# Gate and up of 20 row pairs as block products of seven, two pairs direct, and the down projection in one group of 22 over rows kept in DRAM

## The chip, the cores and the metric

One core of a Trainium2 chip runs the kernel. The time is that of the device in microseconds (us), the median of several executions. PE is TensorE, DVE is VectorE, ACT is ScalarE, POOL is GpSimd; SP issues all DMAs of this kernel, in one queue.

## The reference, cut to what matters

All is float32, 1024 prompt rows and 8 sample rows (T = 1032 columns in the kernel, which keeps everything transposed, features on partitions).

```python
merged = sum(gates[:, :, n] * (br @ w_branch[n]) for n, br in enumerate((a_out, s_out, c_out)))
h = layer_norm(ALPHA * x + merged @ w_out, ln1_g, ln1_b)          # ALPHA = 2 ** 0.25
gt, up = jnp.split(h @ w_gate_up, 2, axis=-1)                      # 1024 x 2 * 2816
h = layer_norm(ALPHA * h + (jax.nn.silu(gt) * up) @ w_down, ln2_g, ln2_b)   # 2816 x 1024
```

Before these lines stand the combined input projection, a gated linear recurrence and two attentions.

## The kernel before

**Three matmuls per product.** Every operand is split into a high part in the matmul's format and a low rest: `split` (L69-73) is one cast on ACT and one subtraction on DVE. A product takes high x high, high x low, low x high (`mm3`, L100-109), each with a 128 x 128 stationary tile. A list-scheduling planner orders each engine's instructions at build time by the order of the code and by when buffers come free; on the chip each queue then runs in that order.

**Weights.** `half_raw` (L80) loads 512 columns (256 KB) into one of 6 buffers; `half_pair` gives 5 high and 4 low buffers for its split. `weights` does this for a whole row tile.

**The projection** (`project`, to 677 us) already multiplies in blocks of seven. Two row tiles of weights (a pair) and the inputs are cut in 2 x 2 blocks; seven products of sums of blocks stand for eight (`fast_quarter`, `fast_step`, L222-279). Each product runs over two quarters of 258 columns, 4 k tiles and 3 matmuls; the weights' sums and splits are made three steps ahead.

**Branches and out projection.** Each of the three branches loads its input rows from DRAM (`load_branch`, L116) in three column chunks of 384, 384 and 264, multiplies by its weights and adds into `M`. The last one leaves `merged` split in the slots of pool `slots0`. `out_proj` (L993) runs chunk by chunk over 8 output tiles with w_out held in `slots1`, adds ALPHA x, and starts the chunk's `layer_norm`, whose steps are issued between later products (`norm_step`). Its `emit` writes h split into `slots0`, and POOL leaves ALPHA h in `accs`.

**The feed-forward part** (`ffn`, L1030). For each of 22 pairs `gate_up` makes gate and up, 8 k tiles each, per chunk, and the gated row tile, split, stays in `slots1`. As 22 do not fit, there are three groups of 8, 7 and 7 pairs (`FPARTS`). After each of the first two, w_down's columns of that group are loaded once and the partial products of all chunks are added to `accs` (tiles `d`). The last group's w_down is held in `slots0` (tiles `dl`) and run chunk by chunk, with the second norm's steps in between; the last chunk has its own `last_layer_norm` (L932), and the second chunk's norm has a late step that follows it (L987-989).

Of the kernel before, what the change touches and what calls it, by code (L numbers as in the profile page):

```python
# [18 lines left out]
P = 128  # L19
# [5 lines left out]
CH = ((0, 384), (384, 384), (768, 264))  # L25
# [28 lines left out]
class Builder:  # L54
# [61 lines left out]
    def load_branch(self, br, c):  # L116
# [3 lines left out]
        for k in range(KT):  # L120
            hi, lo = (self.slot(e, c, f"b{br}{e}{k}_{c}", br == "s") for e in "HL")
            self.nc.sync.dma_start(lo.bitcast(F32), self.scr[br][:, k, t0:t0 + n])
            self.split(hi, lo, lo.bitcast(F32))
            act[k][c] = (hi, lo)


    def setup(self):
# [10 lines left out]
        nc.vector.memset(self.shift.bitcast(F32), -2.0 / 256)  # L138
# [83 lines left out]
    def fast_quarter(self, st, i):  # L222

        nc, ((a11, a12), (a21, a22)), u = self.nc, st["raw"], st["u"]
        if i in (1, 2, 4, 5):
            src = self.w1.tile([P, D // 2], F32, tag="sum", name=f"us{u}_{i}", bufs=3)
# [357 lines left out]
    def product(self, step, br, m, c, wb, gate):  # L584
# [11 lines left out]
        if step == 2:  # L596
            hi, lo = (self.slot(e, c, f"m{e}{m}_{c}", 0) for e in "HL")
# [288 lines left out]
    def col_mean(self, s, n, name):  # L886

        nc = self.nc
        hi = self.ph.tile([P, 384], F32R, tag="lh", name=f"{name}h", bufs=1)[:, :n]
        lo = self.ph.tile([P, 384], F32R, tag="ll", name=f"{name}l", bufs=1)[:, :n]  # L890
# [6 lines left out]
    def layer_norm(self, c, r, s1, gcol, emit, name, late=False):  # L897
# [6 lines left out]
        s2 = ph.tile([P, 384], F32, tag="s2", name=f"{name}s2{c}", bufs=1)[:, :n]  # L904
        for m in range(KT):
            nc.vector.tensor_sub(r[m], r[m], mu)
            sq = s2 if m == 0 else ph.tile([P, 384], F32, tag="sq", name=f"{name}sq{c}_{m}", bufs=2)[:, :n]
# [5 lines left out]
        rs = ph.tile([P, 384], F32, tag="rs", name=f"{name}rs{c}", bufs=1)[:, :n]  # L913
# [18 lines left out]
    def last_layer_norm(self, n, r, product, gcol, emit):  # L932
# [4 lines left out]
        tile_ = lambda tag, name, bufs, dt=F32: ph.tile([P, 384], dt, tag=tag, name=name, bufs=bufs)[:, :n]  # L937
# [16 lines left out]
        for m in range(KT):  # L954
# [6 lines left out]
            nc.vector.scalar_tensor_tensor(r[m], ps, 0.5, r[m], op0=ALU.mult, op1=ALU.add)  # L961
# [4 lines left out]
            elif m == LATE - 1:  # L966
# [4 lines left out]
                for k in range(LATE):  # L971
                    nc.vector.scalar_tensor_tensor(r[k], c0, 0.5, r[k], op0=ALU.mult, op1=ALU.add)
# [20 lines left out]
    def out_proj(self, merged):  # L993
        nc, io, ph = self.nc, self.io, self.ph
        self.accs = [self.acc.tile([P, T], F32, tag="acc", name=f"acc{m}", bufs=8) for m in range(KT)]
        h = [[None] * 3 for _ in range(KT)]
        self.norm = None
        w = [None] * KT
        for c, (t0, n) in enumerate(CH):
            s1 = ph.tile([P, 384], F32, tag="s1", name=f"o1s{c}", bufs=1)[:, :n]  # L1000
            rs = []
            for m in range(KT):
                if c == 0:
                    w[m] = self.resident(io["wout"][m], KT, f"wo{m}", 1)
# [3 lines left out]
                xr = ph.tile([P, 384], F32, tag="xres", name=f"xres{m}_{c}", bufs=3)[:, :n]  # L1008
# [10 lines left out]
            def emit(m, v, c=c):  # L1019
                bias = self.vec[:, V_B1 + m:V_B1 + m + 1]  # L1020
                hi, lo = (self.slot(e, c, f"h{e}{m}_{c}", 0) for e in "HL")
                nc.scalar.activation(hi, v, AF.Identity, bias=bias)
                nc.vector.scalar_tensor_tensor(lo, v, bias, hi.bitcast(F32), op0=ALU.add, op1=ALU.subtract)  # L1023
# [4 lines left out]
        return h  # L1028

    def ffn(self, h):  # L1030
        nc, io, ph = self.nc, self.io, self.ph

        def gate_up(f, c, wg, wu, j):
            t0, n = CH[c]
            pg = self.mm_tile(wg, h, c, f"fg{f}_{c}", tag=("s", "t")[c % 2])
            self.norm_step()
            t = ph.tile([P, 384], F32, tag="gt", name=f"ft{f}_{c}", bufs=3)[:, :n]
            nc.scalar.activation(t, pg, AF.Tanh, scale=0.5)  # L1038
            nc.vector.scalar_tensor_tensor(t, t, 1.0, pg, op0=ALU.add, op1=ALU.mult)  # L1039
            pu = self.mm_tile(wu, h, c, f"fu{f}_{c}")  # L1040
            nc.vector.tensor_mul(t, t, pu)  # L1041
            hi, lo = (self.slot(e, c, f"g{e}{f}_{c}", 1) for e in "HL")
# [235 lines left out]
```

## Time and profile before

| | us |
|---|---|
| median of 3 runs | 2026.82 |
| lowest, highest | 2025.91, 2030.33 |
| span of the profiled execution | 2027.6 |

How the time divides, by the first starts of the tiles named:

| stage | from, us |
|---|---|
| projection | 6.1 |
| attentions with branches a and c | 681.4 |
| branch s | 1077.2 |
| out projection | 1167.6 |
| gate and up of 8 pairs | 1259.8 |
| down of the first group | 1445.1 |
| down of the last group | 1928.6 |
| end | 2027.6 |

The page gives busy time by engine and groups of instructions; the views used below are the windows (busy time of each engine in a stretch), the timeline (instructions in order of time) and the tiles. A row of the timeline has the start, the length, the engine, the line, the operation, what it writes and reads, the shape, and in brackets how long the engine sat idle before it and what released it.

### The profile page before, as it was taken

The numbers are of one execution on the slowest core, as the hardware profiler recorded it, in microseconds if no ns is written. First come the engines' busy times: TensorE is split into PE (matmuls) and PEld (weight loads), VectorE is DVE, ScalarE is ACT, GpSimd is POOL, SyncE is SP. The second block draws the span as 40 slices with busy tenths as digits, with TensorE's granted clock in tenths as the row PEclk, the third lists the DMA queues.
The fourth block names the chain that finished last, engine by engine and source line by source line (L and its number), as shares of the span: only waits on it lengthen the run. The fifth ranks groups of instructions, "written<-read, shape, count | busy, mean of one in ns | idle before, by whom it ended". The sixth has DMA issues, their size and how long they took to land.

```text
span 2027.6 us, 35380 instructions
## 1 busy us (share of the span) xinstructions
PE 1963.3 (97%) x13732; PEld 1930.0 (95%) x13732; DVE 1204.2 (59%) x2565; ACT 879.1 (43%) x1922; POOL 125.3 (6%) x164
## 2 busy tenths in 40 slices
PE   6899999999999999999999999999999999999997
PEld 5899999999999898988999999999999999999996
DVE  8597888777676555389886568533322332223357
ACT  5456565555656455388774244422201221122324
POOL 3000010100000000012110003100000000000001
PEclk8999999999999999999999999999999999999999
DMA  4365455462333676567525241111211111111102
GB/s 173 129 227 181 153 186 170 144 228 82 118 131 114 234 240 215 158 170 204 155 72 174 85 145 30 43 42 43 58 47 43 42 57 41 57 45 43 56 28 84
DMA packets 140439, 235.41 MB, mean 116 GB/s; under 512 B 17280, under 2 KB 69584, under 8 KB 140240
## 3 DMA queue, kind: packets, MB, share of 16 engines
q1 hardware_dynamic: 140272, 233.17, 36.2%
q8 instruction: 107, 1.75, 0.4%
q14 instruction: 60, 0.49, 0.1%
HBM read 179.95 MB, written 55.23 MB: 116 GB/s over the span
## 4 chain that ended last, share of the span: by engine, by line
PE 86%; DVE 6%; DMA 3%; ACT 3%; issue 1%; SPq 0%; ACTq 0%; DVEq 0%; POOL 0%; POOLq 0%
PE ub L245 5%; PE ub L244 5%; PE ub L246 5%; PE fg L105 4%; PE fg L106 4%; PE fg L107 4%; PE fu L107 4%; PE fu L105 4%; PE fu L106 4%; PE d L105 3%; PE d L107 3%; PE d L106 3%; PE ud L246 2%; PE ud L245 2%; PE ud L244 2%; PE brs L105 1%
## 5 line engine op out<-in xcount | busy, mean ns | idle before, releaser
L105 PE MATMUL fg<-hH,wfg_h 128*128 128x384 f32 (+1 forms) x528 | 168.3, 319 | 3.0 <-DVE acc L1012 1.7
L106 PE MATMUL fg<-hL,wfg_h 128*128 128x384 f32 (+1 forms) x528 | 167.7, 318 | 0.4 <-DVE hL L1023 0.4
L107 PE MATMUL fu<-hH,wfu_l 128*128 128x384 f32 (+1 forms) x528 | 167.7, 318 | 0.0
L106 PE MATMUL fu<-hL,wfu_h 128*128 128x384 f32 (+1 forms) x528 | 167.6, 317 | 0.0
L105 PE MATMUL fu<-hH,wfu_h 128*128 128x384 f32 (+1 forms) x528 | 167.5, 318 | 0.0
L107 PE MATMUL fg<-hH,wfg_l 128*128 128x384 f32 (+1 forms) x528 | 167.5, 317 | 0.0
L1041 DVE TENSOR_TENSOR ft<-ft,fu 128x384 f32<-128x384 f32 (+1 forms) x66 | 33.8, 513 | 139.1 <-PE fu L107 139.1
L105 PE MATMUL d<-gH,wd_h 128*128 128x384 f32 (+1 forms) x360 | 114.4, 318 | 0.0
L106 PE MATMUL d<-gL,wd_h 128*128 128x384 f32 (+1 forms) x360 | 114.2, 317 | 0.0
L107 PE MATMUL d<-gH,wd_l 128*128 128x384 f32 (+1 forms) x360 | 114.2, 317 | 0.0
L1039 DVE SCALAR_TENSOR_TENSOR ft<-ft,fg 128x384 f32<-128x384 f32 (+1 forms) x66 | 33.8, 513 | 135.2 <-ACT ft L1038 132.9
L71 ACT CAST gH<-ft 128x384 fp32r<-128x384 f32 (+1 forms) x66 | 31.7, 481 | 175.0 <-DVE ft L1041 175.0
L105 PEld LDWEIGHTS fg<-hH,wfg_h 128*128 128x128 f32 x528 | 99.1, 188 | 3.9 <-DVE acc L1012 2.0
L106 PEld LDWEIGHTS fg<-hL,wfg_h 128*128 128x128 f32 x528 | 99.2, 188 | 1.0 <-DVE hL L1023 0.9
L107 PEld LDWEIGHTS fg<-hH,wfg_l 128*128 128x128 f32 x528 | 99.3, 188 | 0.0
L107 PEld LDWEIGHTS fu<-hH,wfu_l 128*128 128x128 f32 x528 | 99.2, 188 | 0.0
L105 PEld LDWEIGHTS fu<-hH,wfu_h 128*128 128x128 f32 x528 | 99.2, 188 | 0.0
L106 PEld LDWEIGHTS fu<-hL,wfu_h 128*128 128x128 f32 x528 | 99.2, 188 | 0.0
L1061 DVE SCALAR_TENSOR_TENSOR acc<-d,acc 128x384 f32<-128x384 f32 (+1 forms) x48 | 24.8, 516 | 108.4 <-PE d L107 108.4
L1038 ACT ACTIVATE ft<-fg 128x384 f32<-128x384 f32 (+1 forms) x66 | 30.1, 456 | 134.8 <-PE fg L107 134.8
L244 PE MATMUL ub<-th,u_0h 128*128 128x258 f32 x240 | 69.4, 289 | 7.5 <-ACT th L71 6.1
L244 PE MATMUL ud<-th,u_1h 128*128 128x258 f32 x240 | 70.2, 293 | 6.3 <-ACT u_1h L71 5.2
(957 smaller groups left out, 6872.4 us busy)
## 6 DMA issues: line engine op xcount, KB each, us to landing
ur<-win SPq DMA_DIRECT2D x120, 256.0 KB, 3.6
dck<-cmk SPq DMA_DIRECT2D x32, 256.0 KB, 3.6
dcv<-cmvT SPq DMA_DIRECT2D x32, 256.0 KB, 4.5
st<-scr_q SPq DMA_DIRECT2D x32, 256.0 KB, 5.2
scr_g<-za SPq DMA_DIRECT2D x12, 516.0 KB, 5.8
scr_g<-zb SPq DMA_DIRECT2D x12, 516.0 KB, 3.7
x<-xQ SPq DMA_DIRECT2D x8, 516.0 KB
scr_a<-ge SPq DMA_DIRECT2D x8, 516.0 KB
```

The lines of the kernel that those rows point to most:

```text
L71: ins = self.nc.scalar.copy(hi, src).ins
L105: nc.tensor.matmul(ps, sh, mh, start=i == 0, stop=False)
L106: nc.tensor.matmul(ps, sh, ml, start=False, stop=False)
L107: self.last_mm = nc.tensor.matmul(ps, sl, mh, start=False, stop=closes and i == last).ins
L244: mm(sh[:, w], xh, start=opens and k == 0, stop=False)
L245: mm(sh[:, w], xl, start=False, stop=False)
L246: self.last_mm = mm(sl[:, w], xh, start=False, stop=k == 3).ins
L1038: nc.scalar.activation(t, pg, AF.Tanh, scale=0.5)
L1039: nc.vector.scalar_tensor_tensor(t, t, 1.0, pg, op0=ALU.add, op1=ALU.mult)
L1041: nc.vector.tensor_mul(t, t, pu)
L1061: nc.vector.scalar_tensor_tensor(a, ps, 0.5, a, op0=ALU.mult, op1=ALU.add)
```

## The change

- The chunks become 388, 386 and 258 columns; the last is one quarter.
- h, merged and the inputs of branches a and c are kept in fixed tiles `HL` (774 columns and a tail of 258) instead of slots. The first norm's `emit` leaves h itself in `accs`, without POOL; ALPHA is multiplied where down adds.
- Pairs 0 and 1 are multiplied directly, in four quarters, right behind the out projection (`direct_units`). Beside them `h_sums` makes the sums of blocks of h and splits them.
- Pairs 2 to 21 are block products of seven (`units`, `unit_step`) with `fast_quarter`'s sums of weights.
- Gated rows are stored to a DRAM tensor `f`. `down` loads them again (`rows`), 22 for the first chunk and then 3 per product, splits them, and multiplies all 22 k tiles in one group per chunk and output tile; w_down is loaded and split again for every chunk (`streamed`).

```diff
-CH = ((0, 384), (384, 384), (768, 264))
+CH = ((0, 388), (388, 386), (774, 258))
 ...
-FPARTS = ((0, 8), (8, 7), (15, 7))
+DIRECT = (0, 1)
 ...
-LAST_CH = ((0, 0, 384), (1, 0, 384), (2, 0, 264))
 ...
+    def hl(self, k, t0, n):
+        cut = CH[2][0]
+        main, tail = self.HL[k]
+        return [a[:, t0 - cut:t0 - cut + n] for a in tail] if t0 >= cut else [a[:, t0:t0 + n] for a in main]
 ...
+            if br == "s":
+                hi, lo = (self.slot(e, c, f"b{br}{e}{k}_{c}", 0) for e in "HL")
+            else:
+                hi, lo = self.hl(k, t0, n)
 ...
-        nc.vector.memset(self.shift.bitcast(F32), -2.0 / 256)
+        nc.vector.memset(self.shift.bitcast(F32), -1.0 / 256)
 ...
-            hi, lo = (self.slot(e, c, f"m{e}{m}_{c}", 0) for e in "HL")
+            hi, lo = self.hl(m, t0, n)
 ...
-            nc.vector.scalar_tensor_tensor(r[m], ps, 0.5, r[m], op0=ALU.mult, op1=ALU.add)
+            nc.vector.scalar_tensor_tensor(r[m], r[m], ALPHA, ps, op0=ALU.mult, op1=ALU.add)
 ...
-                    nc.vector.scalar_tensor_tensor(r[k], c0, 0.5, r[k], op0=ALU.mult, op1=ALU.add)
+                    nc.vector.tensor_add(r[k], c0, r[k])
 ...
-            def emit(m, v, c=c):
-                bias = self.vec[:, V_B1 + m:V_B1 + m + 1]
-                hi, lo = (self.slot(e, c, f"h{e}{m}_{c}", 0) for e in "HL")
-                nc.scalar.activation(hi, v, AF.Identity, bias=bias)
-                nc.vector.scalar_tensor_tensor(lo, v, bias, hi.bitcast(F32), op0=ALU.add, op1=ALU.subtract)
-                nc.gpsimd.tensor_scalar(v, v, bias, ALPHA, op0=ALU.add, op1=ALU.mult)
-                h[m][c] = (hi, lo)
+            def emit(m, v, t0=t0, n=n):
+                hi, lo = self.hl(m, t0, n)
+                nc.scalar.activation(v, v, AF.Identity, bias=self.vec[:, V_B1 + m:V_B1 + m + 1])
+                self.split(hi, lo, v)
 
             self.norm_start(self.layer_norm(c, rs, s1, V_G1, emit, "n1"))
 ...
+    def direct_units(self):
+        nc, io = self.nc, self.io
+        def held(src, n, name):
+            out = []
+            for e in range(2):
+                raw = self.half_raw(src[:, e * 512:(e + 1) * 512], 512, f"{name}r{e}_")
+                hi, lo = (self.tp.tile([P, HT], F32R, tag="t", name=f"{name}{x}{e}_", bufs=32)[:, :512] for x in "hl")
+                self.split(hi, lo, raw)
+                out += [(hi[:, i:i + P], lo[:, i:i + P]) for i in range(0, 512, P)]
+            return out
+        def piece(f, q, wg, wu):
+            o = slice(q * QN, (q + 1) * QN)
+            act = [self.hl(k, q * QN, QN) for k in range(KT)]
+            pg, pu = (self.bank(tag, f"f{x}{f}_{q}")[:, :QN] for tag, x in ((("s", "t")[q % 2], "g"), ("mm", "u")))
+            self.mm3(pg, list(zip(wg, act)))
             self.norm_step()
+            t = self.w1.tile([P, QN], F32, tag="gt", name=f"ft{f}_{q}", bufs=2)
             nc.scalar.activation(t, pg, AF.Tanh, scale=0.5)
             nc.vector.scalar_tensor_tensor(t, t, 1.0, pg, op0=ALU.add, op1=ALU.mult)
+            self.mm3(pu, list(zip(wu, act)))
+            nc.vector.scalar_tensor_tensor(t, pu, 0.5, t, op0=ALU.mult, op1=ALU.mult)
+            nc.sync.dma_start(self.scr["f"][:, f, o], t)
+        w = {}
+        for f in DIRECT:
+            make = self.weights if f == 0 else held
+            w[f] = [make(io["wgu"][x + f], D, f"wf{x}_{f}") for x in (0, NF)]
+        self.ht = [[None] * 4 for _ in range(7)]
+        for n, m, q in ((0, 0, 0), (3, 4, 0), (5, 4, 2)):
+            self.ht[n] = [[self.hl(m + k, (q + p) * QN, QN) for p in range(2)] for k in range(4)]
+        for q in range(4):
+            for f in DIRECT:
+                piece(f, q, *w[f])
+            yield
+    def h_sums(self, i):
+        nc = self.nc
+        def pair(i, k, src, sign=1.0):
+            hi, lo = (self.tp.tile([P, HT], F32R, tag="t", name=f"h{i}_{k}{x}", bufs=32) for x in "hl")
+            self.ht[i][k] = [(hi[:, o:o + QN], lo[:, o:o + QN]) for o in (0, QN)]
+            (self.split if sign > 0 else partial(self.split_scaled, scale=sign))(hi, lo, src)
+        wide = lambda name, k: self.cb.tile([P, HT], F32, tag="w", name=f"{name}{k}", bufs=6)
+        x = lambda kh, th, k: self.accs[4 * kh + k][:, th * HT:(th + 1) * HT]
+        if i == 2:
+            self.t2 = [None] * 4
+        for k in range(4):
+            if i == 1:
+                t1 = wide("t1", k)
+                nc.vector.tensor_sub(t1, x(0, 0, k), x(0, 1, k))
+                pair(1, k, t1)
+            elif i == 2:
+                t3, t2 = wide("t3", k), wide("t2", k)
+                nc.vector.tensor_sub(t3, x(1, 1, k), x(0, 1, k))
+                nc.vector.tensor_add(t2, t3, x(0, 0, k))
+                pair(2, k, t2, -1.0)
+                pair(4, k, t3)
+                self.t2[k] = t2
+            else:
+                t4 = wide("t4", k)
+                nc.vector.tensor_sub(t4, self.t2[k], x(1, 0, k))
+                pair(6, k, t4)
+    def unit_step(self, st, i):
+        nc, f = self.nc, st["u"]
+        small = lambda tag, p: self.w2.tile([P, QN], F32, tag=tag, name=f"{tag}{f}_{p}", bufs=2)
+        for p in range(2):
+            if i == 0:
+                st["b", p] = self.bank("mm", f"fb{f}_{p}")[:, :QN]
+            elif i == 1:
+                st["d", p] = self.bank("t", f"fd{f}_{p}")[:, :QN]
+            elif i == 3:
+                st["c", p] = self.bank("s", f"fc{f}_{p}")[:, :QN]
+            b, c, d = st.get(("b", p)), st.get(("c", p)), st.get(("d", p))
+            ps = {0: b, 1: d, 2: b, 3: c, 4: b, 5: d, 6: b}[i]
+            opens = i in (0, 1, 3)
+            sh, sl = st["q", i]
+            mm = partial(nc.tensor.matmul, ps, skip_group_check=not opens)
+            for k in range(4):
+                w = slice(k * P, (k + 1) * P)
+                xh, xl = self.ht[i][k][p]
+                mm(sh[:, w], xh, start=opens and k == 0, stop=False)
+                mm(sh[:, w], xl, start=False, stop=False)
+                self.last_mm = mm(sl[:, w], xh, start=False, stop=k == 3).ins
+            if i == 3:
+                st["za", p], st["t", p] = (self.w2.tile([P, HT], F32, tag="z", name=f"{x}{f}_{p}", bufs=5) for x in ("za", "ft"))
+            za, t = st.get(("za", p)), st.get(("t", p))
+            lo_, hi_ = slice(0, QN), slice(QN, HT)
+            if i in (0, 1, 2):
+                st["s", i, p] = small(("p1s", "p5s", "u2s")[i], p)
+                if i == 1:
+                    nc.scalar.mul(st["s", i, p], ps, 0.5)
+                else:
+                    nc.scalar.copy(st["s", i, p], ps)
+            elif i == 3:
+                nc.vector.tensor_add(za[:, lo_], c, st["s", 0, p])
+            elif i == 4:
+                st["zb", p] = small("zb", p)
+                nc.vector.scalar_tensor_tensor(st["zb", p], b, -0.5, st["s", 1, p], op0=ALU.mult, op1=ALU.subtract)
+            elif i == 5:
+                nc.vector.tensor_add(za[:, hi_], d, st["s", 2, p])
+                nc.scalar.activation(t, za, AF.Tanh, scale=0.5)
+                nc.vector.scalar_tensor_tensor(t, t, 1.0, za, op0=ALU.add, op1=ALU.mult)
+                nc.vector.tensor_mul(t[:, hi_], t[:, hi_], st["zb", p])
+            else:
+                nc.vector.scalar_tensor_tensor(t[:, lo_], b, -0.5, t[:, lo_], op0=ALU.mult, op1=ALU.mult)
+                dst = self.scr["f"][:, f, :].rearrange("p (h q n) -> p h q n", h=2, q=2)[:, :, p, :]
+                nc.sync.dma_start(dst, t.rearrange("p (h n) -> p h n", h=2))
+    def units(self):
+        io, st = self.io, {}
+        def load(f):
+            st[f] = self.fast_load(f, io["wgu"][f], io["wgu"][NF + f])
+            st[f]["load"]((0, 0), (0, 1), (1, 0), (1, 1))
+        todo = [(f, i) for f in range(NF) if f not in DIRECT for i in range(7)]
+        ahead = 3
+        load(todo[0][0])
+        for f, i in todo[:ahead]:
+            self.fast_quarter(st[f], i)
+        yield
+        for n, (f, i) in enumerate(todo):
+            if i == 1 and f + 1 < NF:
+                load(f + 1)
+            if n + ahead < len(todo):
+                v, j = todo[n + ahead]
+                self.fast_quarter(st[v], j)
+            self.unit_step(st[f], i)
+            if i == 6:
+                del st[f]
+        yield
+    def streamed(self, m, act, ps, closes=True):
+        nc = self.nc
+        for k0 in range(0, NF, 4):
+            n = min(4, NF - k0)
+            w = self.weights(self.io["wdn"][m][:, k0 * P:(k0 + n) * P], n * P, f"wd{act[0][2]}_{m}_{k0}")
+            for j, (sh, sl) in enumerate(w):
+                k = k0 + j
+                mh, ml = act[k][:2]
+                nc.tensor.matmul(ps, sh, mh, start=k == 0, stop=False)
+                nc.tensor.matmul(ps, sh, ml, start=False, stop=False)
+                self.last_mm = nc.tensor.matmul(ps, sl, mh, start=False, stop=closes and k == NF - 1).ins
+    def rows(self, f, c):
+        t0, n = CH[c]
+        hi, lo = (self.gd.tile([P, CH[0][1]], F32R, tag="g", name=f"g{x}{f}_{c}", bufs=84)[:, :n] for x in "hl")
+        self.nc.sync.dma_start(lo.bitcast(F32), self.scr["f"][:, f, t0:t0 + n])
+        self.split(hi, lo, lo.bitcast(F32))
+        return hi, lo, c
+    def down(self):
+        nc, io, ph = self.nc, self.io, self.ph
+        self.norm = None
+        act = [[None] * NF for _ in CH]
+        pending = deque((f, c) for c in range(3) for f in range(NF))
+        def fetch(n):
+            for _ in range(n):
+                if pending:
+                    f, c = pending.popleft()
+                    act[c][f] = self.rows(f, c)
+        fetch(NF)
+        for c, (t0, n) in enumerate(CH):
             rs = [self.accs[m][:, t0:t0 + n] for m in range(KT)]
+            def product(m, last=True, c=c, n=n):
+                ps = self.bank(("mm", "s")[m % 2], f"dl{m}_{c}")[:, :n]
+                self.streamed(m, act[c], ps, last)
+                fetch(3)
                 return ps
 
             def emit(m, v, scale=1.0, t0=t0, n=n):
                 nc.scalar.activation(v, v, AF.Identity, bias=self.vec[:, V_B2 + m:V_B2 + m + 1], scale=scale)
                 nc.sync.dma_start(io["o_y"][:, m, t0:t0 + n], v)
 
+            if c == 2:
                 self.last_layer_norm(n, rs, product, V_G2, emit)
                 break
+            s1 = ph.tile([P, 388], F32, tag="s1", name=f"o2s{c}", bufs=1)[:, :n]
             for m, r in enumerate(rs):
                 ps = product(m)
                 if m in NORM_AT:
                     self.norm_step()
+                nc.vector.scalar_tensor_tensor(r, r, ALPHA, ps, op0=ALU.mult, op1=ALU.add)
                 if m == 1:
                     nc.vector.tensor_add(s1, rs[0], r)
                 elif m > 1:
                     nc.vector.tensor_add(s1, s1, r)
+            self.norm_start(self.layer_norm(c, rs, s1, V_G2, emit, "n2", c == 1))
 
 ...
+                  "q": [P, KT, 2, TP], "k": [P, 2, 2, TP], "v": [P, 8, 512], "f": [P, NF, T]}
 ...
+        self.sums = 2
 ...
+        with pool("acc") as self.acc:
+            with pool("slots0", "right") as slots0:
+                hy = ExitStack()
+                tails = [hy.enter_context(pool("hy")), slots0]
+                cut = CH[2][0]
+                self.HL = [([slots0.tile([P, cut], F32R, name=f"HL{k}{e}") for e in "hl"],
+                            [tails[k // 4].tile([P, T - cut], F32R, name=f"HT{k}{e}") for e in "hl"]) for k in range(KT)]
+                self.M = [self.acc.tile([P, T], F32, tag="acc", name=f"M{m}", bufs=8) for m in range(KT)]
 ...
                     self.load_branch("s", 0)
                     fill(4)
                     for _ in self.branch(2, "s"):
                         pass
+                with pool("ph5") as self.ph:
+                    self.out_proj(self.merged)
+                    late.close()
+                    self.tp = late.enter_context(pool("tp2", "right"))
+                    self.w1 = late.enter_context(pool("ea", "right"))
+                    direct = self.direct_units()
+                    next(direct)
+                with pool("cb") as self.cb:
+                    next(direct)
+                    self.h_sums(1)
+                    next(direct)
+                    self.h_sums(2)
+                    next(direct)
+                    units = self.units()
+                    next(units)
+                    self.h_sums(6)
+                hy.close()
+                with pool("w2") as self.w2:
+                    next(units)
+                late.close()
+            with pool("ph6") as self.ph, pool("gd", "right") as self.gd:
+                self.down()
```

More of the change, by code (lines that the diff above doesn't have):

```diff
@@ L1106, in build, with fill @@
             self.project()
+        self.sums = 2
         self.act, self.merged = {}, [[None] * 3 for _ in range(KT)]
[L1108 to L1124 removed]
+        with pool("acc") as self.acc:
[6 more added lines that the diff above has]
+                self.M = [self.acc.tile([P, T], F32, tag="acc", name=f"M{m}", bufs=8) for m in range(KT)]
+                with ExitStack() as gp:
+                    self.gp = gp.enter_context(pool("gp"))
+                    jobs = chain(self.branch(0, "a"), self.branch(1, "c"))
+                    def fill(n):
+                        for _ in range(n):
+                            next(jobs, None)
+                    with pool("ph1") as self.ph, pool("dp2") as self.dp:
+                        self.mem_attention(fill)
+                    with pool("ph2") as self.ph:
+                        self.windows(fill)
+                    late = ExitStack()
+                    self.slots = [late.enter_context(pool("slots1", "right"))]
                     self.load_branch("s", 0)
```

83 lines of the change are left out of this document (11 added, 72 removed).

## The prediction

> **What bounds the kernel now.** I read the page first (span, busy shares, the chain by engine), then the windows for the stages, the first and last starts of the tiles for where a stage ends, and the timeline for spacings. On the page, the span, the busy line and the chain by engine:
>
> ```profile
> span 2027.6 us, 35380 instructions
> ...
> PE 1963.3 (97%) x13732; PEld 1930.0 (95%) x13732; DVE 1204.2 (59%) x2565; ACT 879.1 (43%) x1922; POOL 125.3 (6%) x164
> ...
> PE 86%; DVE 6%; DMA 3%; ACT 3%; issue 1%; SPq 0%; ACTq 0%; DVEq 0%; POOL 0%; POOLq 0%
> ```
>
> PE is the bound in the mean. Whether it is in the stages that change, the windows tell (columns: PE, PEld, DVE, ACT, POOL busy, granted clock, DMA share, GB/s):
>
> ```profile
> 30.00:680.00 650.00, 632.42 (x5165) 627.42 (x5164) 495.97 (x1007) 360.46 (x680) 42.37 (x50) 0.99 0.45 152
> ...
> 1238.00:1300.00 62.00, 58.53 (x394) 56.65 (x393) 50.70 (x99) 30.40 (x59) 15.34 (x16) 1.00 0.10 30
> 1300.00:1445.00 145.00, 145.00 (x938) 145.00 (x937) 46.85 (x85) 34.16 (x66) 0.00 (x0) 1.00 0.16 47
> ...
> 1771.00:1928.00 157.00, 157.00 (x1007) 157.00 (x1006) 53.72 (x107) 39.70 (x85) 0.00 (x0) 1.00 0.17 49
> 1928.00:1990.00 62.00, 62.00 (x365) 62.00 (x364) 35.92 (x73) 16.03 (x35) 0.00 (x0) 1.00 0.14 47
> ```
>
> From 1300 to 1990 PE never rests, at full granted clock, while DMA is busy 14 to 17%. Fewer streamed columns there shorten the end one for one. The first row is the projection, which already multiplies in blocks of seven: there PE rests 17.6 of 650 us with DVE at 76%.
>
> **What a product costs.** A busy PE is not its rate, so I take starts of neighbours. In the timeline of PE, two half-products of a unit (258 columns) up to the next instruction, one out-projection product (384), and one down product (264):
>
> ```profile
> 300.96 0.28 PE L244 MATMUL ub<-th,u_2h 128*128 128x258 f32 x1
> ...
> 303.84 0.32 PE L105 MATMUL g<-xch,wgh 128*128 128x344 f32 x1
> ...
> 1201.00 0.35 PE L105 MATMUL op<-mH,wo0H 128*128 128x384 f32 x1
> ...
> 1205.18 0.34 PE L893 MATMUL n1mu0p<-n1mu0h,ones 128*128 128x384 f32 x1
> ...
> 2007.59 0.28 PE L105 MATMUL dl<-gH,wdl7H 128*128 128x264 f32 x1
> ...
> 2010.13 0.28 PE L959 MATMUL dl<-c0h,shift 128*128 128x264 f32 x1
> ```
>
> 24 matmuls in 2.88 us are 0.120 us each; 24 in 4.18 are 0.174; 21 in 2.54 are 0.121. The last gate-up group checks this; the starts of the two down tiles stand in their rows:
>
> ```profile
> L107 PE MATMUL d<-gH,wd_l x360: 282/334/337, 1445.5 to 1771.1; 128*128 128x384 f32 x120, 128*128 128x264 f32 x60
> ...
> L105 PE MATMUL dl<-gH,wdl0H x21: 281/334/346, 1928.6 to 1990.1; 128*128 128x384 f32 x14, 128*128 128x264 f32 x7
> ```
>
> Seven pairs take 1928.6 - 1771.1 - 0.1 = 157.4 us, 22.5 each; from spacings 48 x (0.174 + 0.174 + 0.121) = 22.5. They agree.
>
> **(a) Twenty pairs in blocks of seven.** A unit is 7 products x 2 column quarters x 4 k x 3 = 168 matmuls of 258 columns: 168 x 0.120 = 20.16 us. Gain 20 x (22.5 - 20.16) = **-46.8 us**.
>
> [...]
>
> **(b) Two direct pairs** go in quarters: 2 x 4 x 48 = 384 matmuls x 0.120 = 46.1 us for 45.0: **+1.1**.
>
> **(c) Widths 388, 386, 258** for 384, 384, 264. By the slope between 258 and 384 columns, (0.174 - 0.120) / 126, a set of three takes about 0.4705 us for 0.469. 528 sets in down, and some 768 before it (three branches and the out projection, 192 each): up to **+2**, at least 0.
>
> **(d) Do units keep 0.120?** DVE and ACT prices, from the last unit of the projection, which no side job disturbs, and the weights after it:
>
> ```profile
> 656.39 0.69 DVE L72 TENSOR_TENSOR u_3l<-ur,u_3h 128x512 fp32r<-128x512 f32 x1 [1.92 <-PE ub L246]
> ...
> 665.00 0.69 DVE L72 TENSOR_TENSOR u_6l<-ur,u_6h 128x512 fp32r<-128x512 f32 x1 [2.18 <-PE ub L246]
> 666.37 0.43 DVE L271 TENSOR_TENSOR za<-uc,p1s 128x258 f32<-128x258 f32 x1 [0.68 <-PE uc L246]
> ...
> 668.16 0.68 DVE L72 TENSOR_TENSOR wba_l<-wba0r__8961,wba_h 128x512 fp32r<-128x512 f32 x1
> ```
>
> Three steps in 8.61 us, 2.87 each, are 24 x 0.120: a unit alone runs at PE's pace. A new unit asks of DVE 4 sums and 7 splits at 0.69 and, for each of two quarters, five ops at 0.43 and one of 516 at about 0.69: 7.6 + 5.7 = 13.3 us of 20.16, 66%. Bounds 0 and the projection's idle share (2.7% of 403 = 11 us); nearest is the undisturbed unit, and I take **+2**. The result's store (516 KB per unit) meets a DMA busy some 15%: nothing, unless it delays the next unit's loads, which have a whole unit's time.
>
> **(e) From norm to units.** Now PE rests three times there, on the norms (timeline of PE, then the end of the last of them on DVE):
>
> ```profile
> 1263.54 0.44 PE L105 MATMUL fg<-hH,wfg_h 128*128 128x384 f32 x1 [1.70 <-DVE acc L1012]
> 1280.70 0.39 PE L105 MATMUL fg<-hH,wfg_h 128*128 128x264 f32 x1 [1.26 <-ACT hH L1022]
> 1284.39 0.39 PE L106 MATMUL fg<-hL,wfg_h 128*128 128x264 f32 x1 [0.36 <-DVE hL L1023]
> ...
> 1286.73 1.03 DVE L1023 SCALAR_TENSOR_TENSOR hL<-acc,vec,hH 128x264 fp32r<-128x264 f32 x2
> ```
>
> The direct pieces (5.76 us each, two per quarter) reach quarter 3 only 34.6 us after 1263.5, at 1298: the last chunk's norm, due now at 1280.7, has 17 us to spare, so 1.6 us of waits go. Late next is DVE with the sums of h: 32 ops of 516 columns at about 0.69 are 22 us, the first unit's sums and splits 7.6, the second pair's splits 2.8, gating the four pieces left 8 x 0.43 = 3.4. That is 36 us between the norm's end at 1287 and step 6 of the first unit, 46.1 + 17.3 us after 1263.5, at 1327: 40 us. It fits narrowly. Taking POOL's multiplication away shortens the norm a little, at no count. Bounds -1.6 and +10 (a quarter of the 36 us late); I take **+1**.
>
> **(f) The seam from units to down.** Nothing covers it: rows for all 22 k come back from DRAM into space that the units' operands hold to the end. The nearest rows are at the projection's end, where the next stage's rows come from DRAM behind the last unit (SP's queue, ACT, PE's loads, then windows):
>
> ```profile
> 676.94 0.33 SPq L1158 DMA_DIRECT2D scr_g<-zb  x1
> 677.32 4.16 SPq L122 DMA_DIRECT2D baL<-scr_a  x8
> ...
> 680.86 0.51 ACT L71 CAST baH<-baL 128x384 fp32r<-128x384 f32 x1 [1.39 <-DMA baL<-scr_a]
> ...
> 681.42 0.29 PEld L105 LDWEIGHTS bra<-baH,wba_h 128*128 128x128 f32 x1 [5.25 <-ACT baH L71]
> ...
> 677.00:682.00 5.00, 0.57 (x1) 0.29 (x1) 2.47 (x13) 2.47 (x6) 0.00 (x0) 0.86 0.99 356
> 682.00:688.00 6.00, 6.00 (x21) 5.98 (x21) 5.26 (x13) 4.11 (x12) 0.00 (x0) 0.55 1.01 357
> ```
>
> PE rested 5.25 us; the weights were split before (wba_l at 668.16, above), so the planner pulls weights ahead of blocked rows. 22 rows of 199 KB are 4.37 MB, at 356 GB/s 12.3 us; a first product needs 66 x 0.1757 = 11.6. The last row lands about 1 (drain and store) + 3.5 + 12.3 us after the last unit, its split adds 1, its three matmuls 0.5: the first product ends at 18.3 where 11.6 would do, 6.7 late, and weights for the second product share the DMA (1.44 MB, 4 us). Between 6.7 and 10.7 I take **+9**. Bounds: 2 if the first rows find space before the end; 19 if weights queue behind all rows (16 us of rows, a landing, a split).
>
> The 682:688 row shows the clock at 0.55 after that rest. [...]
>
> **(g) Streaming w_down three times.** 8 x 3 products each load 5.5 halves again: 34.6 MB for 11.5, and 3 rows per product. A product takes 11.6 us and needs 2.04 MB, 176 GB/s; in the third chunk 66 x 0.120 = 7.9 us and 1.44 MB, 182 GB/s. Rows for that load, for the end of the kernel, and for the landing of a half:
>
> ```profile
> 1163.00:1185.00 22.00, 22.00 (x136) 22.00 (x135) 17.30 (x43) 14.51 (x36) 0.00 (x0) 1.00 0.85 273
> ...
> 1990.00:2028.00 38.00, 23.18 (x175) 21.36 (x173) 31.28 (x59) 18.16 (x38) 9.12 (x11) 0.88 0.20 71
> ...
> ur<-win SPq DMA_DIRECT2D x120, 256.0 KB, 3.6
> ```
>
> At 273 GB/s PE missed nothing. Six raw buffers, each held for 3.6 us and two splits (1.3), give a half per 0.8 us; the third chunk needs one per 1.44. DVE is tighter there: 44 splits at 0.69 are 30 us beside the norms, which cost 31 us in the last window: 61 of 63 + 15 us, 78%, like the projection. At its 2.7% idle, **+2**; bounds 0 and 10.
>
> **(h) The end.** In DVE's timeline the second chunk's late norm stands in the last one's way.
>
> ```profile
> 2001.42 2.55 DVE L917 RECIPROCAL n2rs<-n2rs 128x384 f32<-128x384 f32 x1 [1.09 <-ACT n2rs L914]
> ...
> 2011.11 1.62 DVE L919 SCALAR_TENSOR_TENSOR acc<-acc,vec,n2rs 128x384 f32<-128x384 f32 x2
> 2012.65 0.42 DVE L961 SCALAR_TENSOR_TENSOR acc<-dl,acc 128x264 f32<-128x264 f32 x1
> ...
> 2019.32 0.51 DVE L919 SCALAR_TENSOR_TENSOR acc<-acc,vec,n2rs 128x384 f32<-128x384 f32 x1
> ```
>
> The last product ended at 2010.4, its accumulation started at 2012.65 behind two of them, another sits at 2019.32: 2.0 + 0.5 us. The third chunk is now 63 us long instead of 20, so that norm is over before: **-2.5**. Bounds -4 and 0 (the planner leaves it last).
>
> **The sum:** -46.8 + 1.1 + 2 + 2 + 1 + 9 + 2 - 2.5 = **-32.2 us**. The profiled execution's span of 2027.6 becomes 1995.4; it lies 0.8 above the median of 2026.82. Predicted: **1995.0**.
>
> **Rivals.**
> - *The seam is nearly hidden* (rows find space early, +2; streaming costs 0, the units 0): 1995.4 - 7 - 2 - 2 = 1984. For it: the planner hoists. Against: the last unit's step 6 reads its operand tiles up to its last matmul, and 677.32 came behind the last store. Chance 0.13.
> - *Seam and sums are dear* (weights behind rows +10 more, sums +5, streaming +4): 1995.4 + 19 = 2014. For it: SP issues in order. Against: 668.16. Chance 0.18.
> - *Slower: the weight stream starves.* SP has one queue, and a row load that waits for a free slot (42 pairs of slots, 22 + 24 asked for in the first chunk) holds the halves queued behind it. Each of 24 products then waits for a landing, a cast (0.6, by the 0.51 of 384 columns) and a split, 3.6 + 0.6 + 0.7 = 4.9 us: 118 us, 2113. It decides from 32.2 / 24 = 1.3 us per product. Against: six raw buffers and the 273 GB/s row. Chance 0.06.
> - *The change doesn't do what it says:* units wait on DVE's drains and take a pair's 22.5 us. The gain of 46.8 goes: 2042. Against: the 2.87 us steps. Chance 0.03.
> - *No change*, by losses of 28 to 36 us spread over the seam, the sums and the stream: 2027. Chance 0.04.
>
> **How the numbers follow.** My forecast has 0.56 (1988 to 2004 alone). With the first rival's middle and the second's up to 2018 the range is 1982 to 2018, some 0.82. Faster by over 0.2% (4 us, about what a measurement of this kernel tells from none): 0.56 + 0.13 + 0.18 = 0.87; within 0.04; slower 0.09.
>
> **What would show it.** Right: units' steps 2.88 us apart with PE full; one PE rest of 5 to 6 us at the seam and a first down product of 12 to 18 us; later products at 11.6 and 7.9 us; the second chunk's norm over before the last product. Wrong: a rest before most down products (starvation), PE idle inside units on DVE, or a rest of over 15 us at the seam.

## The result, and the profile after

| | before | after |
|---|---|---|
| median, us | 2026.78 (4 runs) | 2015.27 (4 runs) |
| lowest, highest | 2025.91, 2030.33 | 2012.21, 2015.78 |
| span of the profiled execution | 2027.6 | 2014.0 |

The ratio is 0.9936, 95% interval 0.9922 to 0.9950: faster, by 11.5 us where 32 were forecast. On a second chip the same kernel gave 0.9917 (0.9903 to 0.9930).

The busy time on the changed kernel's page:

```profile
PE 1939.9 (96%) x14308; PEld 1898.6 (94%) x14308; DVE 1378.9 (68%) x2893; ACT 1021.6 (51%) x2204; POOL 102.4 (5%) x140
```

PE is busy 23.4 us less than before, but the span fell by only 13.6: PE now rests more. The windows of the changed kernel tell where (units; seam; two stretches of down):

```profile
1308.00:1708.00 400.00, 400.00 (x3332) 400.00 (x3332) 243.96 (x457) 151.31 (x300) 0.00 (x0) 1.00 0.25 79
1708.00:1773.00 65.00, 48.84 (x203) 39.25 (x203) 27.02 (x50) 22.48 (x43) 0.00 (x0) 0.79 0.45 136
1773.00:1857.00 84.00, 83.99 (x474) 83.67 (x474) 53.73 (x100) 41.48 (x83) 0.00 (x0) 1.00 0.61 184
1857.00:1940.00 83.00, 83.00 (x492) 83.00 (x491) 49.55 (x89) 37.37 (x68) 0.00 (x0) 1.00 0.59 173
```

In the units PE is full for 400 of 400 us, and after 1773 in down too. The loss stands in one row, 1708 to 1773. PE's waits in that stretch, by what ended them (us in total, times, longest):

```profile
PE dl L1181 <- ACT gh L75: 12.8, 8, 5.1
PE dl L1183 <- DVE wd_l L76: 2.1, 4, 0.8
PE dl L1181 <- ACT wd_h L75: 1.0, 2, 0.6
PE dl L1182 <- DVE gl L76: 0.2, 1, 0.2
```

`gh` is the split of a gated row, so PE waits for rows, in eight rests and not in one. The queue that loads them is SP's; its timeline behind the last store:

```profile
1712.74 0.49 SPq L1188 DMA_DIRECT2D gl<-scr_f  x1
1713.33 0.65 SPq L86 DMA_DIRECT2D wd_12r__21981<-wdn  x1
1714.08 1.84 SPq L1188 DMA_DIRECT2D gl<-scr_f  x4
1723.02 0.33 SPq L86 DMA_DIRECT2D wd_16r__21999<-wdn  x1
1723.39 1.85 SPq L1188 DMA_DIRECT2D gl<-scr_f  x4
...
1756.50 1.38 SPq L1188 DMA_DIRECT2D gl<-scr_f  x3
1763.96 0.33 SPq L86 DMA_DIRECT2D wd_0r__22167<-wdn  x1
1764.38 0.38 SPq L1188 DMA_DIRECT2D gl<-scr_f  x1
```

The first 13 rows leave one and then four at a time (the fours at 1714.08, 1723.39 and 1732.76, 9.3 us apart), the rest mostly singly, and ahead of each group stands one load of a half of w_down. These halves belong to the second to fourth products, not to the one that PE is at. What SP waits for (1712 to 1760) is named in one row:

```profile
SPq L86 <- DVE wd_l L76: 37.2, 8, 7.1
```

Eight weight loads waited 37.2 us for a split on DVE, the last reader of a raw buffer. The split in turn waits for PE, as the cast of the second product's first half on ACT shows:

```profile
1731.62 0.62 ACT L75 CAST wd_h<-wd_0r__21927 128x512 fp32r<-128x512 f32 x1 [1.84 <-PE dl L1182]
```

The circle closes: the split needs a free half buffer, that needs PE to be through with four k tiles, and for these PE needs rows, which stand in SP's queue behind the load.

The seam can be measured the same way in every kernel: from the last unit's end to the start of the eighth accumulation of the first chunk (DVE's timeline, L1226 here), less 8 products at 11.67 us, the distance of later ones, 93.4 us. The last matmul of the units on PE, then the accumulations on DVE:

```profile
1711.54 0.28 PE L1121 MATMUL fb<-h_3h,u_6l 128*128 128x258 f32 x1
1716.96 0.69 PE L1181 MATMUL dl<-gh,wd_h 128*128 128x388 f32 x1 [5.14 <-ACT gh L75]
```

```profile
1769.30 1.03 DVE L1226 SCALAR_TENSOR_TENSOR acc<-acc,dl 128x388 f32<-128x388 f32 x2 [0.72 <-PE dl L1183]
1777.98 0.56 DVE L1226 SCALAR_TENSOR_TENSOR acc<-acc,dl 128x388 f32<-128x388 f32 x1 [0.37 <-PE dl L1183]
...
1836.38 0.55 DVE L1226 SCALAR_TENSOR_TENSOR acc<-acc,dl 128x388 f32<-128x388 f32 x1
```

The last five products take (1836.38 - 1777.98) / 5 = 11.68 us each. 1836.38 - 1711.66 - 93.4 = **31.3 us**, where 9 were forecast. The first two products end together (x2), 4.92 us after the 22nd row was issued at 1764.38.

### The profile page after: what moved, and what is told of

It reads as the page before. It is cut to its first block, busy times and chain, and to the rows that moved or that the text cites. A ratio compares the mean times of both kernels' runs of the same rounds, so it can differ in the third digit from the quotient of the medians.

```text
span 2014.0 us, 37769 instructions
## 1 busy us (share of the span) xinstructions
PE 1939.9 (96%) x14308; PEld 1898.6 (94%) x14308; DVE 1378.9 (68%) x2893; ACT 1021.6 (51%) x2204; POOL 102.4 (5%) x140
## 4 chain that ended last, share of the span: by engine, by line
PE 83%; DVE 6%; ACT 5%; DMA 5%; issue 2%; SPq 0%; ACTq 0%; DVEq 0%; POOL 0%; POOLq 0%
PE ub L252 5%; PE ub L251 5%; PE ub L253 5%; PE dl L1183 4%; PE dl L1181 4%; PE dl L1182 4%; PE fb L1120 4%; PE fb L1119 4%; PE fb L1121 4%; PE ud L253 2%; PE ud L252 2%; PE ud L251 2%; PE fd L1120 2%; PE fd L1119 2%; PE fd L1121 2%
## 5 line engine op out<-in xcount | busy, mean ns | idle before, releaser
L1181 PE MATMUL dl<-gh,wd_h 128*128 128x388 f32 (+2 forms) x528 | 173.1, 332 | 13.8 <-ACT gh L75 12.8
L1183 PE MATMUL dl<-gh,wd_l 128*128 128x388 f32 (+2 forms) x528 | 172.5, 329 | 4.3 <-DVE wd_l L76 4.1
L1182 PE MATMUL dl<-gl,wd_h 128*128 128x388 f32 (+2 forms) x528 | 173.3, 330 | 0.2 <-DVE gl L76 0.2
L1181 PEld LDWEIGHTS dl<-gh,wd_h 128*128 128x128 f32 x528 | 102.1, 194 | 18.3 <-ACT gh L75 16.5
L1183 PEld LDWEIGHTS dl<-gh,wd_l 128*128 128x128 f32 x528 | 102.7, 195 | 6.8 <-DVE wd_l L76 6.8
L1182 PEld LDWEIGHTS dl<-gl,wd_h 128*128 128x128 f32 x528 | 102.6, 194 | 3.2 <-DVE gl L76 3.0
L251 PE MATMUL ub<-th,u_2h 128*128 128x258 f32 x240 | 69.1, 288 | 5.4 <-ACT th L81 5.4
L252 PE MATMUL ud<-tl,u_1h 128*128 128x258 f32 x240 | 70.2, 293 | 3.1 <-DVE tl L76 3.1
L253 PE MATMUL ud<-th,u_1l 128*128 128x258 f32 x240 | 69.9, 293 | 0.8 <-DVE u_1l L76 0.8
L252 PE MATMUL ub<-tl,u_2h 128*128 128x258 f32 x240 | 69.1, 288 | 0.7 <-DVE tl L82 0.7
```

Of the source, the lines that this page charges most:

```text
L251: mm(sh[:, w], xh, start=opens and k == 0, stop=False)
L252: mm(sh[:, w], xl, start=False, stop=False)
L253: self.last_mm = mm(sl[:, w], xh, start=False, stop=k == 3).ins
L1181: nc.tensor.matmul(ps, sh, mh, start=k == 0, stop=False)
L1182: nc.tensor.matmul(ps, sh, ml, start=False, stop=False)
L1183: self.last_mm = nc.tensor.matmul(ps, sl, mh, start=False, stop=closes and k == NF - 1).ins
```

## The experiments

**Theory Q (the queue):** weight loads of later products stand ahead of row loads in SP's in-order queue, each waits for a raw buffer, and so rows arrive as slowly as PE frees half buffers. **Rivals:** *A*, the order of row and weight splits on ACT and DVE holds PE; *R*, the rows come back from DRAM slowly; *C*, the clock (0.50 in these rests) is the cost itself. The first three runs shared a chip, on which the kernel before had a median of 2030.93.

**1. Rows ahead of the second product's weights.**

```diff
-        self.nc.sync.dma_start(lo.bitcast(F32), self.scr["f"][:, f, t0:t0 + n])
+        self.last_row = self.nc.sync.dma_start(lo.bitcast(F32), self.scr["f"][:, f, t0:t0 + n]).ins
...
-                self.streamed(m, act[c], ps, last)
+                with ExitStack() as behind:
+                    if c == 0 and m == 1:
+                        behind.enter_context(self.tc.issue_after(first))
+                    self.streamed(m, act[c], ps, last)
```

(`first` is `last_row` after the first 22 rows; `issue_after` keeps the block's loads behind it. Both kinds of load are SP's here.)

> The edit: the weight loads of the second down product of the first chunk are kept behind the 22 row loads, in SP's queue; ACT's and DVE's splits of these weights move behind the rows' splits too. Theory Q (a row load waits in SP's queue behind a prefetched weight load, which waits for a raw buffer, which waits for a split, which waits for PE's first k tiles, which wait for rows): the 22 rows issue in about 11 us instead of 47, the first product ends some 18 us after the last unit and the eighth 25 us earlier than now; time 2015.3 - 25 = 1990 us. Theory C (PE at half clock after the rest is what makes the first products long): the row loads move but PE still runs at half clock for some 30 us; gain under 8 us, 2007 to 2015. Theory R (reading the rows back from DRAM is slow in itself): no gain, 2015.

Measured: 1995.72 us (1994.12 to 2000.05), ratio 0.9828 (0.9812 to 0.9845). Its timelines of PE, SP and DVE, and its windows at the seam:

```profile
1717.32 0.28 PE L1121 MATMUL fb<-h_3h,u_6l 128*128 128x258 f32 x1
1722.28 0.69 PE L1181 MATMUL dl<-gh,wd_h 128*128 128x388 f32 x1 [4.68 <-ACT gh L75]
...
1718.51 11.04 SPq L1188 DMA_DIRECT2D gl<-scr_f  x22
...
1820.79 0.55 DVE L1230 SCALAR_TENSOR_TENSOR acc<-acc,dl 128x388 f32<-128x388 f32 x1
```

```profile
1718.00:1724.00 6.00, 1.72 (x4) 1.42 (x5) 1.84 (x5) 1.83 (x5) 0.00 (x0) 0.66 0.94 286
1724.00:1730.00 6.00, 5.18 (x21) 4.42 (x21) 3.60 (x7) 3.86 (x10) 0.00 (x0) 0.77 1.06 384
```

All 22 rows leave in 11.04 us and move at up to 384 GB/s, so R falls. The seam is 1820.79 - 1717.44 - 93.4 = 10.0 us. The rest ahead of the first product is about as long as before (4.68 and 5.14 us) and the clock dips as well (0.66), so a dip behind one rest isn't the cost, and C alone falls. What the changed kernel loses by its granted clock of 0.50 to 0.76 between 1712 and 1748 (windows of 6 us) is not separated from what its rests cost.

**2. Rows on another queue, order otherwise left.** The order of splits on ACT and DVE stays all but the same.

```diff
-        self.nc.sync.dma_start(lo.bitcast(F32), self.scr["f"][:, f, t0:t0 + n])
+        self.nc.gpsimd.dma_start(lo.bitcast(F32), self.scr["f"][:, f, t0:t0 + n])
```

> The edit: the row loads alone are issued by POOL instead of SP; the order of splits on ACT and DVE stays all but that of the changed kernel (the second product's weight splits between the rows' splits). Theory Q (SP's queue): as with the rows first, 1990 to 1995 us. Theory A (it is ACT's and DVE's order that holds the rows: a cast of the second product's weights waits for PE in front of row casts): the rows land early but are split as late as now, 2010 to 2015 us. Theory R (slow reads): 2015 us.

Measured: 1996.80 us, ratio 0.9836 (0.9822 to 0.9851). SP's waits (1709 to 1760), then PE's last unit, POOL's first rows and the eighth accumulation:

```profile
SPq L86 <- DVE wd_l L76: 41.0, 17, 4.6
```

```profile
1712.98 0.28 PE L1121 MATMUL fb<-h_3h,u_6l 128*128 128x258 f32 x1
...
1710.93 4.85 POOL L1188 DMA_DIRECT2D gl<-scr_f  x9 [402.38 <-DMA wd_4r__21945<-wdn]
...
1818.70 0.56 DVE L1226 SCALAR_TENSOR_TENSOR acc<-acc,dl 128x388 f32<-128x388 f32 x1
```

This run parts Q from A. SP's weight loads wait for splits as long as ever, 41.0 us, and it no longer matters, because no row stands behind them: the seam is 1818.70 - 1713.10 - 93.4 = 12.2 us. A falls, since the splits kept their order. Their order still holds the last rows: the 22nd is cast on ACT at 1749.83, over 20 us after its load was issued, and the first two products end together at 1751.65. But PE has matmuls of the second and third products to do meanwhile, and the seam is short.

**3. The other candidate: DVE's burst at the second chunk's norm.**

```diff
-                nc.vector.tensor_add(s2, s2, sq)
+                (nc.gpsimd if late else nc.vector).tensor_add(s2, s2, sq)
```

> The edit: in the second chunk's last norm the seven additions of squares go to POOL, so that a weight split of the third chunk's second product waits behind 4 us of DVE work instead of 6.5. If the 2.05 us rest of PE at 1944 us is this burst, it goes and the time falls by 2 to 3 us, to 2012.5; the seam stays as it is. If POOL and DVE slow each other there, or the burst is not the cause, 2015 us or a little more.

Measured: 2014.58 us, ratio 0.9924 (0.9907 to 0.9941), not told apart from the changed kernel (0.9936 and 0.9917). PE's waits from 1850 to 2001, in the changed kernel and then in this one:

```profile
PE dl L1183 <- DVE wd_l L76: 2.1, 1, 2.1
```

```profile
PE dl L1183 <- DVE wd_l L76: 0.6, 2, 0.3
PE dl L1181 <- ACT wd_h L75: 0.5, 1, 0.5
```

The rest of 2.1 us becomes three short ones of 1.1: about 1 us, below what the runs resolve.

**4. The changed kernel as it is,** the control for runs 5 to 7, which stood beside it on one chip (before: 2029.45).

> The changed kernel once more, as a control on the same chip as the three runs below. By the first comparison 0.9936 of the kernel before, a seam of 31 us beyond PE's own work (eighth accumulation of the first chunk 31 us later than 93.4 us after the units' end).

Measured: 2012.26 us, 0.9917 (0.9903 to 0.9930), seam 1835.21 - 1711.51 - 93.4 = 30.3 us.

**5. Edits 1 and 3 together.**

> Rows ahead of the second product's weights and the late sum of squares on GpSimd, both. If the two costs are independent (the queue at the seam, some 21 us of it avoidable; VectorE's burst at the second chunk's norm, 2 us): 0.9828 less 0.001, so 0.9815 to 0.983, and no PE rest over 1 us between the first chunk's end and the last product. If the rest at the norm only moves: 0.983 and a rest of about 2 us somewhere else in the second chunk.

Measured: 1992.84 us (1990.11 to 1994.72), ratio **0.9817** (0.9803 to 0.9830), seam 9.7 us, and PE's longest rest from 1735 to 1990 is 0.9 us. Run once more, beside run 9 below:

> Rows first on SyncE and the late sum of squares on GpSimd, once more, as the control for the run beside it: 0.9817 and a seam of 9.7 us.

it gave 1993.56 us and 0.9826 (0.9811 to 0.9841), with a seam of 9.8 us. Beside edit 1 alone (0.9828) edit 3 adds nothing that can be measured.

**6. A dose between:** only 11 rows must go first (run 5 with `last_row` taken at the 11th row).

> As e4, but only the first 11 of 22 rows must go ahead of the second product's weights. If each round of weights that stand among rows costs what it did in the changed kernel (9.3 us per group of four rows, up to three rounds for the last 11): seam 15 to 25 us, ratio 0.986 to 0.990. If the first 11 rows give PE enough to free the half buffers meanwhile, as good as e4 (0.982), or better where the second product's weights come earlier.

Measured: 1999.86 us, ratio 0.9856 (0.9842 to 0.9869). Its PE, SP and DVE:

```profile
1709.90 0.28 PE L1121 MATMUL fb<-h_3h,u_6l 128*128 128x258 f32 x1
...
1711.10 5.25 SPq L1188 DMA_DIRECT2D gl<-scr_f  x11
...
1822.34 0.55 DVE L1232 SCALAR_TENSOR_TENSOR acc<-acc,dl 128x388 f32<-128x388 f32 x1
```

Seam 1822.34 - 1710.02 - 93.4 = 18.9 us, between 9.7 and 30.3, as expected of a dose.

**7. Raw buffers of its own for the second product.**

> The changed kernel with six raw buffers of its own for the weights of the second product, nothing reordered by hand. If the row loads are held by weight loads that wait for a raw buffer, the second product's loads no longer hold them: they go out at once (or before the units' end), the first 13 rows leave together, and the seam falls from 31 us to between 10 and 20 (third product's loads may still hold the last rows): ratio 0.983 to 0.989. If what is late is the split's own place on ScalarE and VectorE, or the reading of the rows, nothing changes: 0.993.

The edit asked for names that begin `wd_1_`, and the tiles are called `wd0_1_`, so no buffer changed and the run is a second control: 0.9920 (0.9908 to 0.9933), seam 30.9 us. It says nothing of raw buffers.

**8. The raw buffers again**, with the right names and 76 slots for rows where there were 84.

```diff
-        r = self.wpool.tile([P, D // 2], F32, tag="raw", name=name, bufs=6)
+        if name.startswith("wd0_1_"):
+            r = self.ph.tile([P, D // 2], F32, tag="rawx", name=name, bufs=6)
+        else:
+            r = self.wpool.tile([P, D // 2], F32, tag="raw", name=name, bufs=6)
```

> Six raw buffers of its own for the second product's weights (its halves are named by chunk and product; four pairs fewer for rows make the space, which only the second chunk's rows use). If the row loads are held by weight loads that wait for a raw buffer: no load of the second product waits, all 22 rows leave within 12 to 20 us of the last store, the seam falls from 31 us to 10 to 15, ratio 0.983 to 0.986. If the split's place on ScalarE and VectorE or the reading of rows is what is late: the rows may leave early, but the seam stays near 31 and the ratio near 0.992.

Measured: 2020.08 us, ratio 0.9938 (0.9925 to 0.9951): a miss. Its SP timeline, SP's waits (1709 to 1760), PE's last rest of over 1 us at the seam, and DVE:

```profile
1728.54 0.33 SPq L89 DMA_DIRECT2D wd_16r__22119<-wdn  x1
1728.92 1.85 SPq L1191 DMA_DIRECT2D gl<-scr_f  x4
1737.88 0.33 SPq L89 DMA_DIRECT2D wd_20r__22137<-wdn  x1
1738.26 5.66 SPq L1191 DMA_DIRECT2D gl<-scr_f  x12
1765.33 0.33 SPq L89 DMA_DIRECT2D wd_0r__22167<-wdn  x1
1765.76 0.38 SPq L1191 DMA_DIRECT2D gl<-scr_f  x1
```

```profile
SPq L89 <- DVE wd_l L76: 41.0, 5, 21.4
```

```profile
1741.40 0.69 PE L1184 MATMUL dl<-gh,wd_h 128*128 128x388 f32 x1 [1.97 <-ACT gh L75]
...
1770.67 1.03 DVE L1229 SCALAR_TENSOR_TENSOR acc<-acc,dl 128x388 f32<-128x388 f32 x2 [0.72 <-PE dl L1186]
```

The second product's loads no longer wait, but the planner used the freed buffers to pull the third product's loads (22119, 22137) and one of the fourth's (22167) ahead of rows, and these wait. Counted from the units' end, 21 rows have left after 30.5 us instead of 46.2, and the seam is 31.0 us all the same. The 22nd row, behind a load that waited 21.4 us, holds the end of the first two products (4.91 us after its issue), but it isn't where the time goes: after the rest that ends at 1741.40 PE rests 1.6 us in all up to 1770.67, since it has other products' matmuls. The time was lost earlier. At 24.4 us after the units only 9 rows had left, where 13 had in the changed kernel, and PE's rests add up to 16.4 us, as many as there (16.1). So these buffers alone cured nothing: the planner spent them on more weight loads ahead of the rows that were needed first.

**9. What is left of the seam:** run 5's edits with the rows issued by POOL.

> The two edits of the last good version, with the rows issued by GpSimd instead of SyncE, and the second product's weights still behind all of them. If the first rows wait for the last store on SyncE's queue (with GpSimd they went 0.6 us before the units' end), the first product begins 3 us earlier and the seam falls from 9.7 to 6 to 8: ratio 0.980. If the 22 rows' transfer at 370 to 380 GB/s is what sets the first product's end, only the start moves: seam 9 to 10, 0.9815.

Measured: 1997.64 us (1990.92 to 2000.00), ratio 0.9850 (0.9829 to 0.9871), not told apart from run 5's kernel beside it (0.9811 to 0.9841). The profiled execution is the shortest of the four; its seam is 1812.88 - 1709.59 - 93.4 = 9.9 us. Its PE, SP and DVE, and a window of the seam:

```profile
1709.47 0.28 PE L1121 MATMUL fb<-h_3h,u_6l 128*128 128x258 f32 x1
1710.80 0.44 PE L1181 MATMUL dl<-gh,wd_h 128*128 128x388 f32 x1 [1.05 <-ACT gh L75]
...
1702.21 0.33 SPq L86 DMA_DIRECT2D wd_0r__21927<-wdn  x1
...
1745.85 1.03 DVE L1230 SCALAR_TENSOR_TENSOR acc<-acc,dl 128x388 f32<-128x388 f32 x2 [0.72 <-PE dl L1183]
```

```profile
1714.00:1720.00 6.00, 4.34 (x18) 2.88 (x18) 3.93 (x8) 3.62 (x9) 3.87 (x9) 1.00 1.03 393
```

The order that the expectation counts on did not take hold. (In run 2 the first rows had gone 2.2 us ahead of the units' end, at 1710.93 and 1713.10, and not 0.6.) The second product's first load (21927) leaves SP at 1702.21, ahead of the units' end, where in run 5 it left at 1725.86, behind the 22 rows; and the first two products end together (x2), as in run 2. With the rows on POOL, `issue_after` a row did not hold SP's loads. So this is run 2 with edit 3, and neither expectation was tested: whether rows that start earlier shorten the seam stays open.

Beside run 2, which has the same order at the seam, it shows something else. PE begins after a rest of 1.05 us in both and rests 5.9 us in all in run 2 and 5.7 here. But here the granted clock stays at 1.00 (windows of 6 us from 1708 to 1738) and the seam is 9.9 us; in run 2 the clock fell, and the seam was 12.2:

```profile
1720.00:1726.00 6.00, 5.46 (x15) 4.53 (x15) 3.00 (x8) 2.92 (x8) 3.96 (x8) 0.50 1.03 375
```

The lowest median here is that of run 5's kernel: 1992.84 us, 1.8% under before and below the changed kernel's 2012.26 on the same chip. It is not told apart from run 1's.

## Why the prediction was right in part, and where it was wrong

The two profiled executions, by stage; before, a pair counts 22.5 us:

| stage | before | after | moved | forecast |
|---|---|---|---|---|
| to the out projection | 1167.6 | 1168.2 | +0.6 | - |
| out projection, norm, two direct pairs | 92.2 + 45.0 | 139.9 | +2.7 | +2.1 and part of (c) |
| 20 pairs | 450.0 | 403.6 | -46.4 | -46.8 + 2 |
| down | 255.6 | 288.8 | +33.2 | +11 and part of (c) |
| after the last product | 17.2 | 13.55 | -3.65 | -2.5 |
| sum | 2027.6 | 2014.0 | -13.6 | -32.2 |

(Before's down is 2010.4 - 1259.8 - 22 x 22.5, with the norms' three rests in it. After's stages are cut by the tile `fb` and PE's last matmuls.)

```profile
L1119 PE MATMUL fb<-HL0h,u_0h x40: 280/285/287, 1308.1 to 1692.9; 128*128 128x258 f32 x40
...
2000.33 0.28 PE L967 MATMUL dl<-c0l,shift 128*128 128x258 f32 x1
2000.45 0.60 PE L983 MATMUL le<-ls,ones 128*128 128x258 f32 x2
```

- **(a), (d): right.** 20 units take 1711.66 - 1308.1 = 403.6 us, 20.18 each for a forecast of 20.16. The 2 us set aside for slower units weren't needed.
- **(b), (c), (e): right within 2 us.** Of the norms' rests one of 0.4 us is left. The +2 of (c) has no ground in its own slope: the three widths sum to 1032 columns before and after, so a constant slope gives no difference.
- **(f) failed, and it is the whole miss.** The step took +9 between bounds of 2 and 19; it measured 31.3, outside the bounds, 22.3 us more, of which the other terms made good some 4. What it said of the rows holds once they go first: a rest of 5 us (4.7 and 4.8), rows at up to 384 and 381 GB/s, a seam of 10.0 and 9.7 us (runs 1 and 5). The step that failed is what it drew from "the planner pulls weights ahead of blocked rows". The planner did so, but I read this as weights that have landed, as at the projection's end, put their cost to the rows at nothing, and bounded the opposite case by weights behind rows. The third case was missed: weight loads of later products placed ahead of rows, not yet free to go. The sign that I had named, a rest of over 15 us, came as many rests of 16.1 us in all, the longest 5.1.
- **The dear rival** has the right time by luck: it says 2014, and the span is 2014.0. But it adds weights behind rows, dearer sums and dearer streaming, and what happened is rows behind weights, with the other two as cheap as forecast.
- **The rival that starves** named this very thing, in-order SP with a load that waits for space, the other way round (rows that hold weights) and for all 24 products. It was there to be seen that either kind can hold the other. The weights held the rows, and only until the first two products were through: afterwards PE ran full at 11.67 us per product.
- **The clock:** in the changed kernel the granted clock was 0.50 from 1716 to 1722, after a rest of 5.1 us that ended at 1716.96, and 0.50 between 1730 and 1742, after one of 3.1 us that ended at 1727.32. In run 2 the longest rest at the seam was 1.5 us, and the clock still fell to 0.50. The forecast's sum has no term for the clock, and for run 2's order that is too little: beside run 9 the dip goes with 2.3 us, in one execution each. In the long seam PE's rests make 16.1 of 31.3 us; in the other 15 PE was busy, up to 1748 at a granted clock of 0.50 to 0.76 (windows of 6 us), and how much of them a full clock would save was not tried.
- **(g): right.** +2 was one rest of 2.1 us at the second chunk's norm, by DVE, as named. Behind the seam, at 173 to 184 GB/s, the stream never starved PE.
- **(h): right, 1.15 us better.** PE goes from the last shift (2000.33) to the sums without a rest.

## What to carry to other kernels

When loads of two kinds share one in-order queue, ask of each whether its destination is free when its turn comes. In the changed kernel prefetches that waited for a buffer, 37.2 us in all, held the needed rows behind them in SP's queue, and as that buffer came free only through the held rows, the first groups of four left 9.3 us apart. Put the loads that PE needs next ahead of any prefetch, or on another queue (seams of 10.0 and 12.2 us in runs 1 and 2, for 31.3), before giving the prefetch more buffers (31.0 in run 8); and see in the trace that the order took hold, since in run 9, across two queues, it did not. In this trace it showed as groups of one to four issues with gaps between them at a DMA share of 0.45, and the queue's own waits named the buffer.

## What the runs showed of the hardware

- Loads that could not go yet held the rows behind them in the same queue: in the changed kernel SP waited 37.2 of 48 us on eight issues while the DMA was busy 45% in the seam's window. They did not hold another queue: in run 2 SP waited 41.0 us, and POOL issued the 22 rows within 17 us all the same.
- With rows issued by POOL the DMA moved as much as with SP in the best windows of 6 us (393 GB/s in run 9 and 384 in run 1, weights included). In run 2 nine issues took POOL 4.85 us, 0.54 each, for 0.50 on SP in run 1 (11.04 for 22); but POOL paused between later ones, by up to 2.05 us, so that its 22 rows took 17 us.
- In run 2 the granted clock fell to 0.50 (1720 to 1726) where no rest of PE at the seam was longer than 1.5 us; in run 9, with the same order there, it stayed at 1.00 (1708 to 1738). This is one execution each.
